# Half of the up projection by Strassen's seven block products

## Chip, cores and metric

The kernel runs on one core of a Trainium2 chip. Its time is the device time of one launch in microseconds (us), a median of several runs; lower is better.

## What is computed

One layer of a hybrid encoder on 256 tokens of width 2048: an input projection feeds chunked attention, a diagonal state-space mixer (S5) and an mLSTM; the gated branches are merged, projected and added to x; cross-attention to 256 memory tokens follows, and at the end a gated feed-forward part, which the change touches:

```python
def _swiglu(h, w_gu, w_down):
    g, u = jnp.split(h @ w_gu, 2, axis=-1)
    return (jax.nn.silu(g) * u) @ w_down
...
x = x + _swiglu(_rms(x, norm_ffn[i]), w_gu[i], w_down[i])
```

All arrays are float32; w_gu is 2048 x 11264, w_down 5632 x 2048. On the chip the 256 tokens are two token tiles of 128, and the 2048 rows of w_gu are 16 k-tiles of 128.

## The kernel before

**One product** is `gemm_i` (L120). The activations are the stationary operand, 128 k by 128 tokens; the weights move, 512 columns at a time. To keep float32 accuracy, each operand is the sum of two parts in the type float32r: a high part, the rounded value, and a low part, the rest. A product takes three matmuls: high by high (L146), high by low (L147), low by high (L148), added up in PSUM. For 512 columns and 16 k-tiles that is 16 x 2 token tiles x 3 = 96 matmuls of 512 columns.

**The weights** come from HBM in blocks of four k-tiles, 1 MB, by `load_w` (the DMA is at L101, on the queue of SP) into `raw`, which has two buffers. `split_w` (L110) makes the two parts of each half of a block, called a piece here: two k-tiles, 1024 columns wide in SBUF. ScalarE writes the high part `whi` (the cast, L116), and VectorE the low part `wlo`, raw minus high (the difference, L117):

```python
hi = wp.tile([P, 1024], F32R, tag="whi", name=nm("whi"), bufs=4)
lo = wp.tile([P, 1024], F32R, tag="wlo", name=nm("wlo"), bufs=4)
with tc.high_priority(offset=WPRI):
    S.copy(hi[:, :n], raw[:, c0:c1])
    V.tensor_tensor(lo[:, :n], raw[:, c0:c1], hi[:, :n].bitcast(F32), ALU.subtract)
```

Each has four buffers, so a piece can be made while three earlier ones wait or are read; its cast waits until TensorE has read the piece four before it.

**The feed-forward part** (from L993) has eleven chunks of 512 hidden columns. For each: `gemm_i` for the gate, its result through silu on ScalarE (L1006) into `gt`; `gemm_i` for the up projection, whose result VectorE multiplies into `gt` (L1010); then `to_operand` (L804) transposes `gt` on TensorE (L812) and splits it (L206, L207) into `hT`, the operand of the down projection with 44 k-tiles. After all eleven, four products of w_down follow, and VectorE adds x1 to each result (L1022) and stores it. A gate product and the up product of the same chunk are called a pair here. The operand of gate and up, `x2T`, is made by `to_operand` while the output projection of the cross-attention (w_xo) runs, just ahead of the feed-forward part; there VectorE adds x to its result (L844).

**The order** on each engine is set when the program is built: a scheduler takes the instructions by priority (loads, casts and differences of weights first, then what empties PSUM), and at run time every engine goes through its own list in sequence, each instruction waiting for its semaphores.

Of the kernel before, what the change touches and what calls it, by code (L numbers as in the profile page):

```python
# [9 lines left out]
F32 = mybir.dt.float32  # L10
F32R = mybir.dt.float32r
I32 = mybir.dt.int32
BF16 = mybir.dt.bfloat16
AF = mybir.ActivationFunctionType
# [4 lines left out]
P = 128  # L19
T = 256  # L20
# [11 lines left out]
KF = FF // P  # L32
# [6 lines left out]
# columns of the array of per-partition parameters  # L39
# [8 lines left out]
# columns of the array of constants: identity, ones, mask of the mLSTM  # L48
# [4 lines left out]
def tile_block(ctx: ExitStack, tc: tile.TileContext, a: dict, out: bass.AP):  # L53
# [52 lines left out]
    def dma_after(dst, src):  # L106
        """a load that comes behind the weights asked for so far"""
        with tc.issue_after(last_w[0]):
            nc.sync.dma_start(dst, src)

# [9 lines left out]
    def gemm_i(xh, xl, nk, src, off, n, evac, first=None):  # L120
        """acc[tok, n] = x @ w; w comes from the flat array src at off, in blocks [P, 4, n]."""
# [73 lines left out]
    def rstd_of(dst, ss, n, r=None):  # L195
        """dst = (ss / n + eps) ^ -0.5 (* r, one factor per partition)"""
# [6 lines left out]
    def split_act(hi, lo, src, g=None):  # L203
        """hi + lo = src * g, exactly up to float32."""
# [7 lines left out]
    def transposes(dst, srcs):  # L212
        """dst [P, len * 128] in PSUM: each src [rows, 128] transposed."""
# [10 lines left out]
    # the tensor engine's clock rises while it waits for the first loads  # L224
# [12 lines left out]
    def load_x(k, n=0):  # L237
        """what is wanted of x before the weights of k-tiles k .. k+n-1 of the first product"""
# [20 lines left out]
    def vexp(dst, src, n):  # L259
# [12 lines left out]
        # 2^k in two factors  # L272
# [12 lines left out]
    # =====================  S5  =====================  # L285
# [25 lines left out]
    def s5_params():  # L311
# [5 lines left out]
        # reduce the angle to [-pi, pi]  # L317
# [10 lines left out]
        # (a - 1) / lambda  # L328
# [50 lines left out]
    def powers(tb, c1, s1):  # L379
        """tb[:, :, j, t] = (cos, sin) of t * angle, t < 16; returns nothing."""  # L380
# [4 lines left out]
        for n, m in ((2, 1), (3, 2), (5, 4), (9, 7)):  # L385
            # entries n .. n+m-1 are those 1 .. m turned by entry n-1
# [13 lines left out]
    def s5_gen():  # L400
        """the scan, pair of groups by pair of groups; yields after each step of work"""
# [69 lines left out]
    # =====================  mLSTM  =====================  # L471
# [23 lines left out]
    def mqk(h):  # L495
        """q^T and k^T of head h, [e, tok]"""
# [26 lines left out]
    def m_gates():  # L523
        """decays of the mLSTM: a (tok-major), -c (rows), exp(-m) (tok-major)"""
# [98 lines left out]
    # =====================  chunked attention  =====================  # L623
# [60 lines left out]
    # =====================  gates and branches  =====================  # L684
# [3 lines left out]
    def gate(b, n, dst):  # L688
        """sigmoid of the gate's pre-activation, branch b, columns of chunk n, into dst(t)"""
# [37 lines left out]
    # us  # L727
# [9 lines left out]
    # xm  # L737
# [10 lines left out]
    # vm, with the input and forget gates beside head 0  # L748
# [7 lines left out]
    # attention and om  # L756
# [18 lines left out]
    # gates and branches m and a  # L775
# [30 lines left out]
    def to_operand(srcs, dh, dl, k0, gname=None):  # L806
        """srcs: two tiles [128 tok, 512]; their transpose goes to k-tiles k0 .. k0+3"""
# [328 lines left out]
```

## Time and profile before

| what | value |
|---|---|
| time, median of 3 runs | 2051.26 us (2050.34 to 2051.73) |
| profiled execution, first to last instruction (span) | 2048.7 us |
| busy: TensorE (PE) | 2039.7 us, 100% |
| busy: weight loads of TensorE (PEld) | 1670.9 us, 82% |
| busy: VectorE (DVE) | 1251.7 us, 61% |
| busy: ScalarE (ACT) | 966.0 us, 47% |
| gate and up, all eleven pairs | 1294.1 to 1797.0 us of the span |

The profile is of one execution; its own time is given by the span alone, which leaves out what lies before the first instruction and after the last. The median of the runs is 2.6 us above it. Matmuls overlap in the pipeline and their ends are modelled, so a rate is read from the distance between their starts, not from their durations.

### The profile page before, as it was taken

The page shows a single profiled execution, that of the slowest core. Times are in us where ns is not written, and L with a number is a line of the kernel's source. Part 1 is how long each engine was busy: PE and PEld are TensorE (multiplying, and loading weights), DVE is VectorE, ACT ScalarE, POOL GpSimd, SP SyncE. Part 2 cuts the span into 40 slices and gives each one's busy share as a digit, 9 for nine tenths or more (in the row PEclk, how much of TensorE's full clock was granted, in tenths as well). Part 3 has the DMA queues.
Part 4 walks back from the last instruction along what each step waited for, and adds up shares of the span by engine and source line. Part 5 has one row for each costly group of instructions (what it writes and reads, how often), then busy time and mean ns, then how long its engine had stood idle before and what let it go on. Part 6 is the DMA issues. An engine that isn't in the chain of part 4 may idle for free.

```text
span 2048.7 us, 25114 instructions
## 1 busy us (share of the span) xinstructions
PE 2039.7 (100%) x9880; PEld 1670.9 (82%) x9880; DVE 1251.7 (61%) x1804; ACT 966.0 (47%) x1308; POOL 73.7 (4%) x142
## 2 busy tenths in 40 slices
PE   9999999999999999999999999999999999999999
PEld 7998888777777788888888888888888888888887
DVE  7967885769887857645544655445444444444443
ACT  8555556544344445554544545444444444433332
POOL 1001202000000000011000100000000000000000
PEclk9999999999999999999999999999999999999999
DMA  8555455445555555765555444555555555555553
GB/s 309 186 174 165 152 179 186 155 172 174 180 183 188 192 171 195 271 218 175 175 185 185 144 145 164 185 185 185 185 185 185 185 185 185 185 185 195 195 197 132
DMA packets 60406, 377.78 MB, mean 184 GB/s; under 512 B 6912, under 2 KB 8064, under 8 KB 18816
## 3 DMA queue, kind: packets, MB, share of 16 engines
q1 hardware_dynamic: 56880, 367.42, 51.4%
q0 software_dynamic: 2112, 6.82, 1.2%
q10 hardware_dynamic: 1296, 1.95, 0.3%
q8 instruction: 77, 1.26, 0.2%
q14 instruction: 41, 0.34, 0.1%
HBM read 374.06 MB, written 2.10 MB: 184 GB/s over the span
## 4 chain that ended last, share of the span: by engine, by line
PE 99%; DVE 0%; DMA 0%; issue 0%; SPq 0%; ACT 0%; DVEq 0%; ACTq 0%
PE acc L146 29%; PE acc L148 29%; PE acc L147 28%; PE acc L169 2%; PE acc L170 2%; PE acc L171 2%; PE sm L422 1%; PE sm L812 1%; PE sm L952 1%; PE sm L978 1%; PE sm L449 1%; PE sm L215 0%; PE sm L896 0%; DMA raw<-in_w_in_dram 0%; DVE xT_l L210 0%
## 5 line engine op out<-in xcount | busy, mean ns | idle before, releaser
L117 DVE TENSOR_TENSOR wlo<-raw,whi 128x1024 fp32r<-128x1024 f32 (+2 forms) x700 | 834.7, 1194 | 697.7 <-ACT whi L116 694.3
L116 ACT CAST whi<-raw 128x1024 fp32r<-128x1024 f32 (+2 forms) x700 | 715.9, 1025 | 941.3 <-PE acc L148 816.9
L146 PE MATMUL acc<-whi,x2T_h 128*128 128x512 f32 x704 | 281.2, 399 | 0.0
L148 PE MATMUL acc<-whi,x2T_l 128*128 128x512 f32 x704 | 277.9, 395 | 0.0
L147 PE MATMUL acc<-wlo,x2T_h 128*128 128x512 f32 x704 | 277.2, 394 | 0.0
L147 PE MATMUL acc<-wlo,xT_h 128*128 128x512 f32 (+2 forms) x704 | 264.6, 377 | 1.8 <-DVE wlo L117 1.6
L148 PE MATMUL acc<-whi,xT_l 128*128 128x512 f32 (+2 forms) x704 | 265.3, 378 | 0.0
L146 PE MATMUL acc<-whi,xT_h 128*128 128x512 f32 (+2 forms) x704 | 262.4, 377 | 0.2
L148 PEld LDWEIGHTS acc<-whi,x2T_l 128*128 128x128 f32 x704 | 132.2, 188 | 33.4
L147 PEld LDWEIGHTS acc<-wlo,x2T_h 128*128 128x128 f32 x704 | 132.2, 188 | 31.4
L146 PEld LDWEIGHTS acc<-whi,x2T_h 128*128 128x128 f32 x704 | 132.2, 188 | 30.1
L147 PEld LDWEIGHTS acc<-wlo,xT_h 128*128 128x128 f32 x704 | 132.0, 188 | 29.8 <-DVE wlo L117 3.3
L146 PEld LDWEIGHTS acc<-whi,xT_h 128*128 128x128 f32 x704 | 131.5, 188 | 29.6 <-issue 3.2
L148 PEld LDWEIGHTS acc<-whi,xT_l 128*128 128x128 f32 x704 | 132.1, 188 | 27.8 <-issue 1.9
L146 PE MATMUL acc<-whi,hT_h 128*128 128x512 f32 x352 | 139.1, 395 | 0.0
L147 PE MATMUL acc<-wlo,hT_h 128*128 128x512 f32 x352 | 139.1, 395 | 0.0
L148 PE MATMUL acc<-whi,hT_l 128*128 128x512 f32 x352 | 139.0, 395 | 0.0
L148 PE MATMUL acc<-whi,eT_l 128*128 128x512 f32 x256 | 101.6, 397 | 0.0
L147 PE MATMUL acc<-wlo,eT_h 128*128 128x512 f32 x256 | 101.4, 396 | 0.0
L146 PE MATMUL acc<-whi,eT_h 128*128 128x512 f32 x256 | 101.2, 395 | 0.0
L169 PE MATMUL acc<-xT_h,whi 128*128 128x256 f32 x352 | 99.9, 284 | 0.0
L170 PE MATMUL acc<-xT_l,whi 128*128 128x256 f32 x352 | 99.5, 283 | 0.0
(375 smaller groups left out, 2837.0 us busy)
## 6 DMA issues: line engine op xcount, KB each, us to landing
raw<-in_w_gu_dram SPq DMA_DIRECT2D x88, 1024.0 KB, 4.8
raw<-in_w_in_dram SPq DMA_DIRECT2D x68, 1024.0 KB, 4.8
raw<-in_w_down_dram SPq DMA_DIRECT2D x44, 1024.0 KB, 4.7
raw<-in_w_xkv_dram SPq DMA_DIRECT2D x32, 1024.0 KB, 4.7
raw<-in_w_ii_dram SPq DMA_DIRECT2D x22, 1024.0 KB, 5.0
raw<-in_w_out_dram SPq DMA_DIRECT2D x16, 1024.0 KB, 5.0
raw<-in_w_xq_dram SPq DMA_DIRECT2D x16, 1024.0 KB, 4.8
raw<-in_w_xo_dram SPq DMA_DIRECT2D x16, 1024.0 KB, 4.8
```

The source lines that it names most:

```text
L116: S.copy(hi[:, :n], raw[:, c0:c1])
L117: V.tensor_tensor(lo[:, :n], raw[:, c0:c1], hi[:, :n].bitcast(F32), ALU.subtract)
L146: PE.matmul(o, sh, h, start=(kt == 0), stop=False)
L147: PE.matmul(o, sh, lw, start=False, stop=False)
L148: PE.matmul(o, xl[:, kt, t * P:(t + 1) * P], h, start=False, stop=(kt == nk - 1))
L169: PE.matmul(po, h, xh[:, kt, :], start=(kt == 0), stop=False)
L170: PE.matmul(po, h, xl[:, kt, :], start=False, stop=False)
L171: PE.matmul(po, lo[:, j * P:(j + 1) * P], xh[:, kt, :], start=False, stop=(kt == nk - 1))
L422: PE.matmul(pb[:, i * T:(i + 1) * T], bT[q:q + 32, i, c, :], u[q:q + 32, c, :], start=True, stop=True, tile_position=(q, 0))
L449: PE.matmul(py[q:q + 32, :], cT[:, i, 4 * c + j, :], xs[j][:, i * T:(i + 1) * T], start=(i == 0), stop=(i == 1), tile_position=(0, q))
L812: PE.transpose(px[:, j * T + t * P:j * T + (t + 1) * P], srcs[t][:, (kp + j) * P:(kp + j + 1) * P], ident)
L952: PE.matmul(pS[:, t * T:(t + 1) * T], qx[:, qi, d, t * P:(t + 1) * P], kx[:, ki, d], start=(d + i == 0), stop=(d == 3 and i == 2))
```

## The change

Of the 16 k-tiles of gate and up, the first eight, four pieces (called ordinary below), are computed as before. The last eight form four pairs of k-tiles, and for each pair the two token tiles and two k-tiles make a 2 x 2 block matrix A (A11 and A12 are the first token tile, A21 and A22 the second), the two k-tiles and two halves of 512 columns a 2 x 2 block matrix B (b11, b12, b21, b22, 128 x 256 each). A block of the four pairs is again a piece of 1024 columns.

- **Up** is computed by seven block products in place of eight (Winograd's form of Strassen's method), summed over the four pairs. It needs sums of blocks: those of A (S1 to S4) are made once, those of B by VectorE for every chunk, in place (`wsum`, L115, four of them). Two products are kept (`kept`, L217, a copy by ScalarE), and VectorE adds and subtracts them to the results in PSUM (`v`, L238). Each product of one block is 4 pairs x 3 = 12 matmuls of 256 columns.
- **Gate** is computed by the usual eight block products (`seven=False`), as the operand now lies in blocks.
- The 2 MB of the last eight k-tiles go into a buffer of their own, `sraw`, one for gate and up together; the parts of a block are made at L202 and L203.
- The operand of the blocks and of S1 to S4 is made by `pairs_operand`; `x2S` is its second half.
- **Two parts**: six chunks, their down projection (24 k-tiles), added into x1; then five chunks and theirs (20 k-tiles), added to x1 and stored. `hT` holds at most 24 k-tiles.

```diff
-KF = FF // P
+FF_PARTS = ((0, 6), (6, 11))
...
+    def wsum(dst, src):
+        with tc.high_priority(offset=WPRI):
+            V.tensor_tensor(dst, dst, src, ALU.add)
...
+    def gemm_s(xh, xl, sop, nk, src, off, evac, seven=True):
...
+        raw = spool[0].tile([P, NS * n], F32, tag="sraw", name=nm("sraw"))
+        for i in range(2):
+            load_w(src[off:off + P * 4 * n].rearrange("(p f) -> p f", p=P), 4 * n,
+                   raw[:, i * 4 * n:(i + 1) * 4 * n])
+            off += P * 4 * n
+        rv = raw.rearrange("p (i q h c) -> p q h i c", q=2, h=2, c=256)
+        b11, b12, b21, b22 = (rv[:, q, h] for q in range(2) for h in range(2))
+
+        def parts(b):
+
+            hi = wp.tile([P, 1024], F32R, tag="whi", name=nm("whi"), bufs=4)
+            lo = wp.tile([P, 1024], F32R, tag="wlo", name=nm("wlo"), bufs=4)
+            hi, lo = (x.rearrange("p (i c) -> p i c", c=256) for x in (hi, lo))
+            with tc.high_priority(offset=WPRI):
+                S.copy(hi, b)
+                V.tensor_tensor(lo, b, hi.bitcast(F32), ALU.subtract)
+            return hi, lo
+
+        def product(o, i, b, start, stop):
+            hi, lo = b
+            for p in range(4):
+                sh, sl = sop(0, p, i), sop(1, p, i)
+                PE.matmul(o, sh, hi[:, p], start=start and p == 0, stop=False)
+                PE.matmul(o, sh, lo[:, p], start=False, stop=False)
+                PE.matmul(o, sl, hi[:, p], start=False, stop=stop and p == 3)
...
+        w21, w22, w11 = parts(b21), parts(b22), None
+        if not seven:
+            w11, w12 = parts(b11), parts(b12)
+            for t in range(2):
+                for h, q, w in ((0, 0, w11), (1, 0, w12), (0, 1, w21), (1, 1, w22)):
+                    product(c(t, h), 2 * t + q, w, False, q == 1 and h == 1)
...
+        product(c(0, 0), A12, w21, False, False)
+        product(c(0, 1), S4, w22, False, True)
+        u1 = kept(side(A11, parts(b11)))
+        v(c(0, 0), c(0, 0), u1, ALU.add)
+        wsum(b11, b12)
+        wsum(b12, b22)
+        wsum(b22, b11)
+        u5 = kept(side(S1, parts(b11)))
+        p6 = side(S2, parts(b22))
+        wsum(b21, b22)
+        v(u1, p6, u1, ALU.add)
+        v(c(0, 1), c(0, 1), u5, ALU.add)
+        v(c(0, 1), c(0, 1), u1, ALU.subtract)
+        evac(0, pp[0])
+        product(c(1, 0), A22, parts(b21), False, True)
+        p7 = side(S3, parts(b12))
+        v(c(1, 1), c(1, 1), u5, ALU.add)
+        v(u1, p7, u1, ALU.add)
+        v(c(1, 0), c(1, 0), u1, ALU.add)
+        v(c(1, 1), c(1, 1), u1, ALU.subtract)
+        evac(1, pp[1])
...
+    def pairs_operand(srcs, n, gname):
...
+            b = pS.tile([P, 8, P], F32, tag="sb", name=nm("sb"), bufs=1)
+            for q in range(2):
+                S.activation(b[:, 0:4].rearrange("p (t q) c -> p q t c", q=2)[:, q],
...
+            V.tensor_tensor(b[:, S1], b[:, A21], b[:, A22], ALU.subtract)
+            V.tensor_tensor(b[:, S3], b[:, A11], b[:, A21], ALU.subtract)
+            V.tensor_tensor(b[:, S2], b[:, S1], b[:, A11], ALU.subtract)
+            V.tensor_tensor(b[:, S4], b[:, S2], b[:, A12], ALU.add)
+            f = b.rearrange("p i c -> p (i c)")
+            split_act(sop(0, pair, 0, 8), sop(1, pair, 0, 8), f)
...
-        off = gemm_i(gTh, gTl, KD, a["w_gu"], off, 512, evg)
-        off = gemm_i(gTh, gTl, KD, a["w_gu"], off, 512, evu)
-        to_operand(sg, hTh, hTl, 4 * n)
...
+    for c0, c1 in FF_PARTS:
+        nk = 4 * (c1 - c0)
...
+            gu_off = gemm_s(gT[0], gT[1], sop, KD, a["w_gu"], gu_off, evg, seven=False)
+            gu_off = gemm_s(gT[0], gT[1], sop, KD, a["w_gu"], gu_off, evu)
+            to_operand(sg, hTh, hTl, 4 * (n - c0))
+        for n in range(4):
+            def ev(t, po, n=n, last=(c1 == FF // 512)):
+                with tc.high_priority(offset=EPRI):
+                    if not last:
+                        d = x1[:, t, n * 512:(n + 1) * 512]
+                        V.tensor_tensor(d, po, d, ALU.add)
+                        return
...
+            gemm_i(hTh, hTl, nk, a["w_down"], (n * FF + c0 * 512) * 512, 512, ev)
```

How the order changes, first on VectorE, in the up product of the second chunk. Before, differences of ordinary pieces follow each other (L117), with the two multiplications of the gate by up (L1010) among them:

```order
L117 TENSOR_TENSOR wlo_11771<-raw_11752,whi_11770 128x1024
L117 TENSOR_TENSOR wlo_11789<-raw_11786,whi_11788 128x1024
L117 TENSOR_TENSOR wlo_11805<-raw_11786,whi_11804 128x1024
L117 TENSOR_TENSOR wlo_11843<-raw_11840,whi_11842 128x1024
L117 TENSOR_TENSOR wlo_11859<-raw_11840,whi_11858 128x1024
L117 TENSOR_TENSOR wlo_11877<-raw_11874,whi_11876 128x1024
L1010 SCALAR_TENSOR_TENSOR gt_11540<-acc_11682,rst,gt_11540 128x512
L1010 SCALAR_TENSOR_TENSOR gt_11541<-acc_11683,rst,gt_11541 128x512
```
Now, line numbers being those of the changed kernel, in the same place, for the blocks of up (L203: difference of a block, L115: sum of blocks, L238: addition of a kept product `u`). `wlo_11974` is of b11, `wlo_11997` of its sum, `wlo_12016` belongs to the fifth product, `wlo_12038` and `wlo_12054` to the sixth and seventh:

```order
L203 TENSOR_TENSOR wlo_11942<-sraw_11938,whi_11941 128x1024
L203 TENSOR_TENSOR wlo_11946<-sraw_11938,whi_11945 128x1024
L203 TENSOR_TENSOR wlo_11974<-sraw_11938,whi_11973 128x1024
L115 TENSOR_TENSOR sraw_11938<-sraw_11938 128x4x256 x2
L203 TENSOR_TENSOR wlo_11997<-sraw_11938,whi_11996 128x1024
L115 TENSOR_TENSOR sraw_11938<-sraw_11938 128x4x256
L238 TENSOR_TENSOR acc_11868<-acc_11868,u_11990 128x256
L115 TENSOR_TENSOR sraw_11938<-sraw_11938 128x4x256
L203 TENSOR_TENSOR wlo_12016<-sraw_11938,whi_12015 128x1024
L238 TENSOR_TENSOR acc_11868<-acc_11868,u_12013 128x256
L203 TENSOR_TENSOR wlo_12038<-sraw_11938,whi_12037 128x1024
L203 TENSOR_TENSOR wlo_12054<-sraw_11938,whi_12053 128x1024
```
The sums and additions stand between the differences, and the addition at L238 of the kept third product is ahead of the fourth sum.

On ScalarE, from gate to up of the same chunk. Before, casts of ordinary pieces (L116) with the silu (L1006) between:

```order
L116 CAST whi_11736<-raw_11718 128x1024
L1006 ACTIVATE gt_11541<-acc_11543,rst 128x512
L116 CAST whi_11754<-raw_11752 128x1024
L116 CAST whi_11770<-raw_11752 128x1024
L116 CAST whi_11788<-raw_11786 128x1024
L116 CAST whi_11804<-raw_11786 128x1024
```
Now, from the third block of the gate's last eight k-tiles (`whi_11762`) over the split of the last chunk's `hT` and the fourth block (`whi_11766`) to the first ordinary piece of up (`whi_11872`):

```order
L202 CAST whi_11762<-sraw_11751 128x1024
L311 CAST hT_h_11267<-sm_11665 128x512
L311 CAST hT_h_11267<-sm_11672 128x512
L202 CAST whi_11766<-sraw_11751 128x1024
L122 CAST whi_11872<-raw_11870 128x1024
```
The first piece of up is the fifth buffer use after the gate's first block, so its cast comes behind the four casts of the gate's blocks.

On TensorE, at the end of the fourth product of up (`whi_11996`), the fifth (`sm_12019`) and the sixth (first into `acc_11869` with `whi_12037`). There was no such place before: `gemm_i` goes piece by piece.

```order
L212 MATMUL sm_12000<-whi_11996,x2S_l 128x256
L210 MATMUL sm_12019<-whi_12015,x2T_h 128x256
L210 MATMUL acc_11869<-whi_12037,x2T_h 128x256
L211 MATMUL sm_12019<-wlo_12016,x2T_h 128x256
L212 MATMUL sm_12019<-whi_12015,x2T_l 128x256
```
And at the end of the fifth, where the seventh (`sm_12057`) begins with one matmul, ahead of the rest of the sixth:

```order
L212 MATMUL sm_12019<-whi_12015,x2S_l 128x256
L210 MATMUL sm_12057<-whi_12053,x2T_h 128x256
L211 MATMUL acc_11869<-wlo_12038,x2T_h 128x256
L212 MATMUL acc_11869<-whi_12037,x2T_l 128x256
```
Of each later product one matmul by the high part is drawn forward; the next needs the low part of the product before it.

## Rows read from the trace of the kernel before

**Rows 1.** The page: busy time by engine, and TensorE's granted clock in forty slices.
```profile
PE 2039.7 (100%) x9880; PEld 1670.9 (82%) x9880; DVE 1251.7 (61%) x1804; ACT 966.0 (47%) x1308; POOL 73.7 (4%) x142
PEclk9999999999999999999999999999999999999999
```
**Rows 2.** The page: the chain that ended last, by engine and by line.
```profile
PE 99%; DVE 0%; DMA 0%; issue 0%; SPq 0%; ACT 0%; DVEq 0%; ACTq 0%
PE acc L146 29%; PE acc L148 29%; PE acc L147 28%; PE acc L169 2%; PE acc L170 2%; PE acc L171 2%; PE sm L422 1%; PE sm L812 1%; PE sm L952 1%; PE sm L978 1%; PE sm L449 1%; PE sm L215 0%; PE sm L896 0%; DMA raw<-in_w_in_dram 0%; DVE xT_l L210 0%
```
**Rows 3.** Busy time by stretch: PE, PEld, DVE, ACT, POOL, granted clock, DMA share, GB/s.
```profile
0.00:3.00 3.00, 1.52 (x4) 1.25 (x5) 0.71 (x6) 0.00 (x0) 0.19 (x4) 1.00 0.38 96
1294.10:1797.00 502.90, 502.90 (x2203) 405.55 (x2203) 245.00 (x225) 212.34 (x227) 1.47 (x4) 1.00 0.52 184
```
**Rows 4.** Timeline at the gate and up projections: start, duration in us, instruction.
```profile
1499.71 0.40 PE L146 MATMUL acc<-whi,x2T_h 128*128 128x512 f32 x1
...
1500.18 0.39 PE L148 MATMUL acc<-whi,x2T_l 128*128 128x512 f32 x1
...
1500.61 1.05 ACT L116 CAST whi<-raw 128x1024 fp32r<-128x1024 f32 x1 [0.71 <-PE acc L148]
...
1501.69 1.22 DVE L117 TENSOR_TENSOR wlo<-raw,whi 128x1024 fp32r<-128x1024 f32 x1 [1.58 <-ACT whi L116]
...
1507.88 0.39 PE L148 MATMUL acc<-whi,x2T_l 128*128 128x512 f32 x1
```
**Rows 5.** Instructions by line and shape, whole span: busy us, mean ns of one.
```profile
L117 DVE TENSOR_TENSOR wlo<-raw,whi 128x1024 fp32r<-128x1024 f32 x658 | 804.2, 1224 | 675.5 <-ACT whi L116 672.3
L308 DVE TENSOR_TENSOR u<-acc,rb 128x256 f32<-128x256 f32 x6 | 2.5, 425 | 1.2 <-PE acc L171 1.0
L844 DVE TENSOR_TENSOR x<-acc,x 128x512 f32<-128x512 f32 x8 | 5.1, 683 | 0.0
L362 DVE TENSOR_TENSOR s2k<-braw,s5p 128x128 f32<-128x128 f32 x6 | 1.7, 284 | 0.0
L116 ACT CAST whi<-raw 128x1024 fp32r<-128x1024 f32 x658 | 688.9, 1049 | 910.6 <-PE acc L148 809.0 <-PE acc L170 27.4 <-DMA raw<-in_w_out_dram 14.5
```
**Rows 6.** Timeline of matmuls of 256 columns and of their weight loads.
```profile
149.90 0.28 PE L146 MATMUL acc<-whi,xT_h 128*128 128x256 f32 x1
...
153.43 0.28 PE L146 MATMUL acc<-whi,xT_h 128*128 128x256 f32 x1
...
150.13 0.19 PEld L146 LDWEIGHTS acc<-whi,xT_h 128*128 128x128 f32 x1
150.25 0.19 PEld L147 LDWEIGHTS acc<-wlo,xT_h 128*128 128x128 f32 x1
```
**Rows 7.** Timeline of single short steps, at three other places.
```profile
6.18 0.69 DVE L117 TENSOR_TENSOR wlo<-raw,whi 128x512 fp32r<-128x512 f32 x1
...
6.92 0.50 PE L147 MATMUL acc<-wlo,xT_h 128*128 128x512 f32 x1 [0.35 <-DVE wlo L117]
7.26 0.39 PE L148 MATMUL acc<-whi,xT_l 128*128 128x512 f32 x1
...
60.90 0.37 ACT L369 COPY s5mats<-sm 128x256 f32<-128x256 f32 x1
...
204.35 0.42 DVE L442 TENSOR_TENSOR xx<-xx,s2k 128x256 f32<-128x256 f32 x1
204.69 0.42 DVE L443 TENSOR_TENSOR xx<-xx,s2k 128x256 f32<-128x256 f32 x1
```
**Rows 8.** DMA: rate in forty slices of the first 40 us; then the page.
```profile
GB/s 0 31 256 276 317 329 302 229 238 301 406 428 397 401 402 410 410 320 299 373 422 434 401 238 385 401 410 426 382 420 449 379 66 123 303 426 397 430 426 418
...
HBM read 374.06 MB, written 2.10 MB: 184 GB/s over the span
...
raw<-in_w_gu_dram SPq DMA_DIRECT2D x88, 1024.0 KB, 4.8
```

More of the change, by code (lines that the diff above doesn't have):

```diff
@@ L109, in dma_after @@
             nc.sync.dma_start(dst, src)
+    spool = [None]
+    def wsum(dst, src):
+        with tc.high_priority(offset=WPRI):
+            V.tensor_tensor(dst, dst, src, ALU.add)
     def split_w(raw, c0, c1):
@@ L989, in tile_block @@
                      resid_evac(n, 2, lambda t: x1[:, t, n * 512:(n + 1) * 512]))
-        to_operand([x1[:, t, n * 512:(n + 1) * 512] for t in range(2)], gTh, gTl, 4 * n,
-                   "norm_ffn")
+        srcs = [x1[:, t, n * 512:(n + 1) * 512] for t in range(2)]
+        if n < 2:
+            to_operand(srcs, gT[0], gT[1], 4 * n, "norm_ffn")
+        else:
+            pairs_operand(srcs, n - 2, "norm_ffn")
     finish_rstd(2, 6)
-    p2.release()
     poolA.release()
     p3 = tc.alloc_tile_pool(name="p3", bufs=1)
-    hTh = p3.tile([P, KF, T], F32R, name="hT_h")
@@ L999, in tile_block @@
-    hTl = p3.tile([P, KF, T], F32R, name="hT_l")
-    off = 0
-    for n in range(FF // 512):
-        sg = [t2k("gt", 2), t2k("gt", 2)]
-        def evg(t, po, sg=sg):
-            with tc.high_priority(offset=EPRI):
-                S.activation(sg[t], po, AF.Silu, scale=rst[:, 6 + t:7 + t])
-        def evu(t, po, sg=sg):
-            with tc.high_priority(offset=EPRI):
-                V.scalar_tensor_tensor(sg[t], po, rst[:, 6 + t:7 + t], sg[t], ALU.mult, ALU.mult)
-        off = gemm_i(gTh, gTl, KD, a["w_gu"], off, 512, evg)
-        off = gemm_i(gTh, gTl, KD, a["w_gu"], off, 512, evu)
-        to_operand(sg, hTh, hTl, 4 * n)
@@ L1014, in tile_block @@
-    off = 0
-    for n in range(4):
-        def ev(t, po, n=n):
-            o = t2k()
-            with tc.high_priority(offset=EPRI):
-                for c in range(0, 512, 256 if n == 3 else 512):
-                    d = slice(c, c + (256 if n == 3 else 512))
-                    g = slice(n * 512 + d.start, n * 512 + d.stop)
-                    V.tensor_tensor(o[:, d], po[:, d], x1[:, t, g], ALU.add)
-                    (nc.sync if c else nc.scalar).dma_start(out[t * P:(t + 1) * P, g], o[:, d])
-        off = gemm_i(hTh, hTl, KF, a["w_down"], off, 512, ev)
+    spool[0] = p3
@@ new lines, in tile_block, with evg, evu @@
+    gu_off = 0
+    for c0, c1 in FF_PARTS:
+        nk = 4 * (c1 - c0)
+        hTh = p3.tile([P, nk, T], F32R, tag="hh", name=nm("hT_h"))
+        hTl = p3.tile([P, nk, T], F32R, tag="hl", name=nm("hT_l"))
+        for n in range(c0, c1):
+            sg = [t2k("gt", 2), t2k("gt", 2)]
+            def evg(t, po, sg=sg):
+                with tc.high_priority(offset=EPRI):
+                    S.activation(sg[t], po, AF.Silu, scale=rst[:, 6 + t:7 + t])
+            def evu(t, po, sg=sg):
+                with tc.high_priority(offset=EPRI):
+                    V.scalar_tensor_tensor(sg[t], po, rst[:, 6 + t:7 + t], sg[t], ALU.mult,
+                                           ALU.mult)
+            gu_off = gemm_s(gT[0], gT[1], sop, KD, a["w_gu"], gu_off, evg, seven=False)
[3 more added lines that the diff above has]
+            def ev(t, po, n=n, last=(c1 == FF // 512)):
+                with tc.high_priority(offset=EPRI):
+                    if not last:
+                        d = x1[:, t, n * 512:(n + 1) * 512]
+                        V.tensor_tensor(d, po, d, ALU.add)
+                        return
+                    o = t2k()
+                    for c in range(0, 512, 256 if n == 3 else 512):
+                        d = slice(c, c + (256 if n == 3 else 512))
+                        g = slice(n * 512 + d.start, n * 512 + d.stop)
+                        V.tensor_tensor(o[:, d], po[:, d], x1[:, t, g], ALU.add)
+                        (nc.sync if c else nc.scalar).dma_start(out[t * P:(t + 1) * P, g],
+                                                                o[:, d])
+            gemm_i(hTh, hTl, nk, a["w_down"], (n * FF + c0 * 512) * 512, 512, ev)
@@ L1025, in tile_block @@
     p3.release()
+    pS.release()
     px1.release()
```

55 lines of the change are left out of this document (53 added, 2 removed).

## Prediction

> **What bounds the kernel now.** I read the page first: busy time by engine, then the chain that ended last, then the stretch of the gate and up projections, then single instructions there. [rows 1, 2] TensorE is busy for 2039.7 of 2048.7 us and is 99% of the chain: nothing else ends late anywhere, so a microsecond of TensorE work saved is a microsecond of time, and a wait put before it is one lost. In the stretch of the 11 gate/up pairs (502.9 us, 45.7 a pair) TensorE is busy throughout, VectorE for 245.0 and ScalarE for 212.3 us [rows 3]. So both have half their time free, but that is an average; what counts is whether a weight piece is ready when TensorE comes to it. [rows 4] show the present beat: 36 matmuls of 512 columns start from 1499.71 to 1507.88, 0.2334 us apart, so a piece of two k-tiles (12 matmuls) takes 2.80 us. The last matmul that reads a piece starts at 1500.18; the cast into its buffer starts at 1500.61, 0.20 after TensorE's next start; the difference follows 0.03 after the cast. Cast and difference take 1.05 and 1.22 us per 1024 columns [rows 5], 2.3 of 2.8 us, with four buffers each: the pieces run three ahead and TensorE never sees them.
>
> **The work on TensorE.** A matmul of 256 columns starts every 0.1177 us (31 from 149.90 to 153.43, each with its own weight load) [rows 6]: half of 512 within 1%, so halving the width costs almost nothing. Gate: 48 matmuls of 512 become 96 of 256: 11.30 for 11.20 us, +0.10. Up: 48 become 84 of 256 (seven products of 12, in place of eight): 9.89 for 11.20, -1.31. The order shows that these counts are really there. Without new waits a pair gains 1.21 us, 13.3 us over eleven.
>
> **The waits, up.** Call 0 the start of the first of the seven products; they take 1.41 us each. The third block's cast reuses the buffer of the third ordinary piece, which TensorE leaves at -2.80; with the 0.20 above it runs from -2.60 to -1.55, its difference to -0.30. Only then may b11 be overwritten: two sums on VectorE. No row has such a sum (1024 columns in four strips, in place). Its bounds are one difference of 1024 columns back to back, 1.14 us (1.22 less the 0.08 by which neighbours overlap), and four adds of 256 columns at 0.42, 1.68 us [rows 5, 7]; I take 1.22, since the differences of the same blocks have the same count and type. The two end at 2.10, the difference of the new b11 at 3.30 (its cast ended at 2.05), the third sum at 4.44. VectorE's next instruction adds the kept third product: that ends on TensorE at 4.24, +0.20, +0.37 for the ScalarE copy [rows 7], so the add runs 4.83 to 5.25 (0.42 [rows 5]). The fourth sum ends at 6.39, the difference for the fifth product at 7.53. TensorE ended the fourth product at 5.65 and has two first-part matmuls (0.24) that need no difference; the rest starts at 7.58 (0.05 from difference to matmul, and about 0.1 more for the first matmul after a wait: 0.34 instead of 0.23 [rows 7]). That is an idle 1.7 + 0.1 = **1.8 us**. The other two differences end at 9.01 and 10.15, before TensorE wants them (9.09 and 10.85). The order of the three queues decides this: each is in sequence, the add stands ahead of the fourth sum, and TensorE has only one matmul each of the next products to go on with.
>
> **The waits, gate to up.** The gate holds its four blocks to the end, because both token tiles use each. The first ordinary piece of up reuses the buffer of the third block, free only after seven of eight products: 84 x 0.1177 + 0.20 = 10.09, cast to 11.14, difference to 12.39, matmul at 12.44. The gate's products ended at 11.30 and one matmul of 0.23 goes ahead: idle 0.91, with the restart **1.0 us**. At the other boundary, up to gate, the first buffers are freed by products long done; nothing is late there.
>
> **Work at nothing.** The additions of kept products after the last product, the silu and the eight extra adds of the first feed-forward part into x1 (0.68 each [rows 5]) fall under ordinary pieces, where VectorE and ScalarE have half their time; the transposes of a pair stand 5 us after its last product, and the chain before them (an add, two differences, two adds, the gating) is about as long, which leaves no more than 0.2 us. The down projection has as many matmuls as before, in 24 + 20 k-tiles. **Loads**: the block buffer of 2 MB is single, and SP issues the next two loads only when the last difference or sum has read it: 10.15 after 0. At the 400 GB/s that the queue reached in the first 40 us, 2.1 MB takes 5.2 us, and an issue-to-landing of 4.8 for 1 MB leaves some 2.2 fixed [rows 8]: landed at 17.6, third cast done at 20.8 to 21.6, while TensorE has the ordinary pieces and transposes until 23.8. Cover 2 us; if it were gone, the wait would follow microsecond for microsecond.
>
> **Once**: the first gate. Its operand for the last k-tile pair is made behind the cast of the fourth block, which waits for the last ordinary piece. From the start of the products: 0.2, cast 1.05, difference 1.22, four sums of 128 columns at 0.28, cast 1.05, difference 1.22 = 5.9 [rows 5]. TensorE has 22 matmuls (2.6 us) that need less: **3.3 us**.
>
> **Sum.** A pair: +0.10 - 1.31 + 1.8 + 1.0 = +1.6; eleven +17.5; with the 3.3, **+20.8 us**. The profiled execution's span is 2048.7, so 2069.5; the runs' median stands 2.6 above the span, so 2072. All hops shorter (sums at 1.14, no restart costs) give +14; sums at 1.68 give 1.8 us more a pair, +41.
>
> **Rivals.** (a) *The blocks are ready in time.* Then the products show their count: 11 x -1.21 + 3.3 = -10, 2041 us. For it: VectorE is idle half the time. Against: the chain above has no slack in it, since every link waits for a buffer or a sum, not for a free engine. The point where it decides: waits per pair must fall from 2.8 to under 1.2 for no loss, to 0.5 to be seen as faster. 0.08; half-way, within the measurement, 0.05. (b) *The block loads come late.* At the mean rate of 184 GB/s [rows 8] 2.1 MB takes 11.4 us, landing is at 23.8 and the third block's difference at 28.2: 4.4 us per pair, 2120. Against it, the queue holds nothing else at that time. 0.04. (c) *The clock falls in the waits.* All forty slices have the full clock, 2.4 GHz, and so has the first 3 us, where TensorE had stood idle for half [rows 1, 3]. Were the last three products of up (36 matmuls) granted 1.2 GHz, they would take 4.2 us longer, 46 in all: 2118. 0.04. (d) *Weight loads become the bound.* A pair's products have 180 loads where 96 were; at the 0.19 us shown for one, laid end to end, 34.2 us for 22.4, +130: 2181. But [rows 6] loads of 0.19 start every 0.118 us, so they overlap. 0.02. The Trainium skill, Perfetto Trace Analysis, section Identifying the Most-Contended Engine, says to judge TensorE's headroom by the busy share of the weight loads, not of the matmuls. By that rule the change spends what is scarce and (d) would come; by the row the loads have room for 256 columns, and the sum stands.
>
> **The numbers.** My forecast has 0.77, and its own range is 2065 to 2092, from the bounds of the sums and hops. Cases (b) to (d) lie above, 0.10; (a) and its half-way case below, 0.13. The range of eight in ten is 2056 to 2092. A difference under 0.2%, 4.1 us, can't be told from none: faster 0.08, same 0.05, slower 0.87.
>
> **What would show it.** Right: TensorE's idle time, nearly none today, comes to some 34 us, in twenty-two pieces, with the difference of the fifth product's block and that of up's first piece as releasers; a pair takes about 47.3 us; VectorE is busy without a gap for 10 us around the products of up; 256-column matmuls start 0.118 apart. Wrong: no such gaps (a); gaps ended by DMA (b); a clock slice under 9 (c); 256-column matmuls 0.19 apart (d). If the waits are shorter than 1.2 us a pair, the step that failed is the chain of sums.

## The result and the profile after

| | before | changed |
|---|---|---|
| median of the runs, us | 2051.49 (2050.34 to 2052.85, 4 runs) | 2067.35 (2066.55 to 2068.12, 4 runs) |
| span of the profiled execution, us | 2048.7 | 2065.9 |

The ratio is 1.0078 (95% interval 1.0064 to 1.0092): 15.9 us slower, where 20.8 were forecast. The first fence is the page of the changed kernel: busy time by engine, granted clock, the chain that ended last, the loads of the block buffer.

```profile
PE 2037.9 (99%) x10804; PEld 1711.8 (83%) x10804; DVE 1377.2 (67%) x1989; ACT 1007.0 (49%) x1367; POOL 73.9 (4%) x142
...
PEclk9999999999999999999999999999999999999999
...
PE 95%; DVE 2%; DMA 1%; ACT 1%; issue 0%; DVEq 0%; ACTq 0%; SPq 0%
...
sraw<-in_w_gu_dram SPq DMA_DIRECT2D x44, 1024.0 KB, 6.8
```

Against [rows 1, 2] TensorE's busy time hardly moved (2039.7 to 2037.9), the clock is full throughout, and the chain now has some 4% of other engines in it. So TensorE computes no more than before; it waits. The view of its waits, in the feed-forward part, says where (instruction, who ended the wait, us in total, times, longest):

```profile
PE acc L210 <- ACT whi L202: 15.3, 11, 1.4
PE acc L210 <- ACT x2S_h L311: 1.4, 1, 1.4
PE acc L211 <- DVE wlo L203: 1.0, 2, 0.8
PE acc L212 <- DVE x2S_l L312: 0.5, 1, 0.5
```

Eleven waits for the cast of a block, one a pair; of the four others three stand at the first gate and one, the shorter of its line, in the fifth pair. The timeline at the second pair's up products, TensorE first, then VectorE, then ScalarE:

```profile
1380.93 0.28 PE L210 MATMUL acc<-whi,x2T_h 128*128 128x256 f32 x1
...
1386.57 0.27 PE L212 MATMUL sm<-whi,x2S_l 128*128 128x256 f32 x1
1386.82 0.38 PE L210 MATMUL sm<-whi,x2T_h 128*128 128x256 f32 x1
1388.59 0.39 PE L210 MATMUL acc<-whi,x2T_h 128*128 128x256 f32 x1 [1.39 <-ACT whi L202]
1388.82 0.28 PE L211 MATMUL sm<-wlo,x2T_h 128*128 128x256 f32 x1
...
1380.67 2.49 DVE L115 TENSOR_TENSOR sraw<-sraw 128x1024 f32<-128x1024 f32 x2
1383.09 1.23 DVE L203 TENSOR_TENSOR wlo<-sraw,whi 128x1024 fp32r<-128x1024 f32 x1
1384.23 1.22 DVE L115 TENSOR_TENSOR sraw<-sraw 128x1024 f32<-128x1024 f32 x1
1385.85 0.43 DVE L238 TENSOR_TENSOR acc<-acc,u 128x256 f32<-128x256 f32 x1 [0.40 <-ACT u L217]
1386.19 1.22 DVE L115 TENSOR_TENSOR sraw<-sraw 128x1024 f32<-128x1024 f32 x1
1387.32 1.22 DVE L203 TENSOR_TENSOR wlo<-sraw,whi 128x1024 fp32r<-128x1024 f32 x1
...
1385.44 0.37 ACT L217 COPY u<-sm 128x256 f32<-128x256 f32 x1 [2.39 <-PE sm L212]
1385.71 1.05 ACT L202 CAST whi<-sraw 128x1024 fp32r<-128x1024 f32 x1
1386.88 0.37 ACT L217 COPY u<-sm 128x256 f32<-128x256 f32 x1
1387.49 1.99 ACT L202 CAST whi<-sraw 128x1024 fp32r<-128x1024 f32 x2 [0.24 <-DVE sraw L115]
```

VectorE works on without a break except the 0.40 us in which it stands before the add of the kept product. The fourth sum ends at 1387.41; from there both the cast of one block (start 1387.49) and the difference of another (1387.32 to 1388.54) run, both end at about 1388.54, and TensorE goes on at 1388.59. Its two starts are 1.77 apart in place of 0.12; with 0.13 lost ahead of the first and 0.11 at the restart that is 1.89 us.

The boundary from gate to up, where a second wait was forecast. The gate's products start at 1404.88:

```profile
1407.84 0.40 PE L210 MATMUL acc<-whi,x2T_h 128*128 128x256 f32 x2
...
1416.35 0.28 PE L212 MATMUL acc<-whi,x2S_l 128*128 128x256 f32 x1
1416.47 0.39 PE L185 MATMUL acc<-whi,x2T_h 128*128 128x512 f32 x1
1416.71 0.40 PE L186 MATMUL acc<-wlo,x2T_h 128*128 128x512 f32 x1
...
1408.03 1.05 ACT L122 CAST whi<-raw 128x1024 fp32r<-128x1024 f32 x1 [1.51 <-PE acc L212]
```

No gap: the first ordinary piece was cast at 1408.03, 8.4 us before TensorE wanted it. It is 0.19 after the start of 1407.84, when the gate's first 24 block matmuls were through: the order on TensorE uses one block for both token tiles first, and its buffer is free then. It is not the block that was filled first. At the first gate, where the blocks come late, the first matmul by a low part (1309.14, shown next) starts 0.05 us after the third difference of a block ends, although the first two had ended at 1306.82:

```profile
1304.46 2.36 DVE L203 TENSOR_TENSOR wlo<-sraw,whi 128x1024 fp32r<-128x1024 f32 x2 [0.84 <-ACT whi L202]
...
1307.87 1.22 DVE L203 TENSOR_TENSOR wlo<-sraw,whi 128x1024 fp32r<-128x1024 f32 x1
```

The three waits that come once are at the first gate; the rows with what preceded them:

```profile
1307.99 0.40 PE L210 MATMUL acc<-whi,x2T_h 128*128 128x256 f32 x2
1309.14 0.39 PE L211 MATMUL acc<-wlo,x2T_h 128*128 128x256 f32 x1 [0.76 <-DVE wlo L203]
...
1311.05 0.28 PE L212 MATMUL acc<-whi,x2S_l 128*128 128x256 f32 x1
1312.73 0.38 PE L210 MATMUL acc<-whi,x2S_h 128*128 128x256 f32 x1 [1.41 <-ACT x2S_h L311]
...
1313.20 0.27 PE L211 MATMUL acc<-wlo,x2S_h 128*128 128x256 f32 x1
1313.99 0.38 PE L212 MATMUL acc<-whi,x2S_l 128*128 128x256 f32 x1 [0.52 <-DVE x2S_l L312]
```

Each start less the normal spacing (two matmuls ahead of the first): 0.91, 1.56 and 0.67, 3.1 us in all. With about 0.1 us more at each of the three restarts, this gate takes 14.98 us where the next takes 11.52: 3.5 us, paid once.

**The account.** A pair takes 46.75 us (from 1341.84 to 1388.59) against 45.69 before, 1.06 more. Its gate products run from 1358.21 to the next ordinary matmul:

```profile
1358.21 0.40 PE L210 MATMUL acc<-whi,x2T_h 128*128 128x256 f32 x2
...
1369.73 0.40 PE L185 MATMUL acc<-whi,x2T_h 128*128 128x512 f32 x1
```

The parts, from starts: 96 gate matmuls in 11.52 (11.20 before), +0.32; 84 up matmuls at 0.120, 10.08, -1.12; the wait, +1.89. That is +1.09. (The gate at 1404.88 above takes 11.59 because it starts right behind a transpose: its second matmul starts 0.20 after its first. Five of the eleven gates take 11.52; the transposes cost the same elsewhere, since the pairs are equally long.) Eleven periods are 11.7; with the 3.5 of the first gate and one more wait in the fifth pair, 0.5, the sum is 15.7. The feed-forward part, from its first matmul to the last of the kernel, grew by 15.7. The runs differ by 15.9, the profiled spans by 17.2; 1.5 of the spans' difference lies ahead of the feed-forward part, which the change hardly touches: the part starts at 1295.9 here, at 1294.4 in the trace of the kernel before, and between 1294.4 and 1295.9 in the runs below.

### The profile page after: what moved, and what is told of

Read it like the earlier page. It is cut to its first block, busy times and chain, and to the rows that moved or that the text cites. A ratio compares the mean times of both kernels' runs of the same rounds, so it can differ in the third digit from the quotient of the medians.

```text
span 2065.9 us, 27248 instructions
## 1 busy us (share of the span) xinstructions
PE 2037.9 (99%) x10804; PEld 1711.8 (83%) x10804; DVE 1377.2 (67%) x1989; ACT 1007.0 (49%) x1367; POOL 73.9 (4%) x142
## 4 chain that ended last, share of the span: by engine, by line
PE 95%; DVE 2%; DMA 1%; ACT 1%; issue 0%; DVEq 0%; ACTq 0%; SPq 0%
PE acc L152 20%; PE acc L154 20%; PE acc L153 20%; PE acc L187 4%; PE acc L186 4%; PE acc L185 4%; PE acc L210 3%; PE acc L212 3%; PE acc L211 3%; PE acc L274 2%; PE acc L275 2%; PE acc L276 2%; PE sm L527 1%; PE sm L917 1%; PE sm L212 1%; PE sm L211 1%
## 5 line engine op out<-in xcount | busy, mean ns | idle before, releaser
L123 DVE TENSOR_TENSOR wlo<-raw,whi 128x1024 fp32r<-128x1024 f32 (+2 forms) x612 | 725.3, 1189 | 511.3 <-ACT whi L122 509.6
L122 ACT CAST whi<-raw 128x1024 fp32r<-128x1024 f32 (+2 forms) x612 | 622.1, 1022 | 717.4 <-PE acc L154 530.0
L203 DVE TENSOR_TENSOR wlo<-sraw,whi 128x1024 fp32r<-128x1024 f32 x121 | 146.0, 1223 | 80.2 <-ACT whi L202 80.2
L202 ACT CAST whi<-sraw 128x1024 fp32r<-128x1024 f32 x121 | 124.6, 1047 | 149.0 <-PE acc L187 76.3
L187 PE MATMUL acc<-whi,x2T_l 128*128 128x512 f32 x352 | 139.7, 397 | 0.0
L186 PE MATMUL acc<-wlo,x2T_h 128*128 128x512 f32 x352 | 139.6, 397 | 0.0
L185 PE MATMUL acc<-whi,x2T_h 128*128 128x512 f32 x352 | 132.7, 395 | 0.0
L276 PE MATMUL acc<-xT_h,wlo 128*128 128x256 f32 x352 | 99.2, 282 | 0.0
```

The source lines that it names most:

```text
L185: PE.matmul(pp[t], sh, h, start=(kt == 0), stop=False)
L186: PE.matmul(pp[t], sh, lw, start=False, stop=False)
L187: PE.matmul(pp[t], xl[:, kt, t * P:(t + 1) * P], h, start=False, stop=False)
L203: V.tensor_tensor(lo, b, hi.bitcast(F32), ALU.subtract)
L276: PE.matmul(po, lo[:, j * P:(j + 1) * P], xh[:, kt, :], start=False, stop=(kt == nk - 1))
```

## The experiments

Theory: the loss is the chain of sums on VectorE, the spacing of the gate's 256-column matmuls, and the first gate's operand. Rivals stand with each run. Base is the changed kernel unless said. Times are medians; the ratio is to the kernel before on the same chip.

**No sums.**

```diff
     def wsum(dst, src):
-        with tc.high_priority(offset=WPRI):
-            V.tensor_tensor(dst, dst, src, ALU.add)
+        return
```

> The changed kernel without the four block sums on VectorE (this leaves out part of the computation: the up projection's seven products use the unsummed weight blocks). Theory 'chain of sums': the gap of TensorE in the seven products of up, 1.65 us from start to start beyond the normal spacing and with its restarts 1.88 us a pair, comes from four sums and a copy-and-add that stand in one queue on VectorE. Without the sums it goes: 2067.4 - 11 x 1.88 = about 2047 us, and TensorE's idle time behind the block casts (15.3 us) falls to under 2 us. Rival 'buffers': the wait is set by the four part buffers and by the 1.05 us casts on ScalarE; then the sums only lie beside it and the time stays within 4 us of 2067.

2045.75 us, 0.9972 (0.9961 to 0.9984): 21.6 less than with them. The waits for block casts are gone from the view; of 15.3 us none is left. The rival falls.

**Another order of the seven products.**

```diff
-        product(c(0, 0), A12, w21, False, False)
-        product(c(0, 1), S4, w22, False, True)
         u1 = kept(side(A11, parts(b11)))
-        v(c(0, 0), c(0, 0), u1, ALU.add)
         wsum(b11, b12)
+        product(c(0, 0), A12, parts(b21), False, False)
+        product(c(0, 1), S4, parts(b22), False, True)
         wsum(b12, b22)
         wsum(b22, b11)
         u5 = kept(side(S1, parts(b11)))
-        p6 = side(S2, parts(b22))
+        p7 = side(S3, parts(b12))
         wsum(b21, b22)
+        p6 = side(S2, parts(b22))
+        v(c(0, 0), c(0, 0), u1, ALU.add)
...
         product(c(1, 0), A22, parts(b21), False, True)
-        p7 = side(S3, parts(b12))
```

> All of the computation, but the seven products of up in another order: A11 by b11 first (so that b11 and b12 are summed while the last ordinary pieces run), the product of S3 ahead of that of S2, the product that needs the fourth sum last, the first add behind the fourth sum. Theory 'chain of sums': it is the place of the sums, not their length, that costs; the sums then begin some 8 us earlier and end before TensorE wants them, the 1.88 us a pair go: 2067.4 - 20.7 = about 2047 us (2046 to 2052), no gap over 0.2 us in the products of up. Rival 'VectorE has no room': seven differences and four sums, 13 us of VectorE in 10 us of products, cannot be hidden by order; the wait moves to another product and the time stays over 2060.

2046.46 us, 0.9975 (0.9965 to 0.9985), all of the computation done: 20.9 us less than the changed kernel, 1.90 a pair, and below the kernel before. VectorE and TensorE at the second pair, whose products start at 1379.40:

```profile
1373.54 1.23 DVE L115 TENSOR_TENSOR sraw<-sraw 128x1024 f32<-128x1024 f32 x1
...
1376.23 1.22 DVE L115 TENSOR_TENSOR sraw<-sraw 128x1024 f32<-128x1024 f32 x1
...
1379.14 1.23 DVE L115 TENSOR_TENSOR sraw<-sraw 128x1024 f32<-128x1024 f32 x1
...
1381.87 1.22 DVE L115 TENSOR_TENSOR sraw<-sraw 128x1024 f32<-128x1024 f32 x1
...
1379.40 0.28 PE L210 MATMUL sm<-whi,x2T_h 128*128 128x256 f32 x1
...
1388.16 0.63 PE L185 MATMUL acc<-whi,x2T_h 128*128 128x512 f32 x2
```

The same four sums; three of them now start ahead of the products, the first 5.9 us ahead. The 73 block matmuls before the next ordinary one take 8.76 us; in the changed kernel as many took 10.64 (1380.93 to 1391.57). The difference is the wait. A pair now takes 44.86 us, 1.89 less than in the changed kernel. So it was not the amount of VectorE's work but its place.

**Without the first add.** One line is left out: `v(c(0, 0), c(0, 0), u1, ALU.add)`.

> The changed kernel without the one VectorE instruction that adds the kept third product to the result (this leaves out part of the computation: that product is missing in the first quarter of up). In the changed kernel this add stands ahead of the fourth block sum and the queue stands still 0.40 us for it and works 0.43 us on it. Theory 'chain of sums': the wait of TensorE shrinks by these 0.83 us a pair: 2067.4 - 11 x 0.83 = about 2058 us, a gap of about 0.8 us left in every pair. Rival 'buffers': an add of 256 columns matters only for its own place; the gap stays 1.65 us and the time within 2 us of 2067.

2063.24 us, 1.0058 (1.0043 to 1.0073): 4.1 less, neither the 9 expected nor nothing. The fourth sum was done 0.70 us earlier beside TensorE's clock, as meant, but the timeline of ScalarE shows the next limit:

```profile
1385.35 1.05 ACT L202 CAST whi<-sraw 128x1024 fp32r<-128x1024 f32 x1
1386.52 0.37 ACT L217 COPY u<-sm 128x256 f32<-128x256 f32 x1
1386.79 2.00 ACT L202 CAST whi<-sraw 128x1024 fp32r<-128x1024 f32 x2
```

The copy of the fourth product stands ahead of the cast that TensorE waits for, and it must itself wait for TensorE. Two runs followed to see whether this queue is the second limit.

**Without copies and additions.** `kept` and `v` do nothing.

> The changed kernel without the copies of the kept products and without the additions of products to the results (this leaves out part of the computation: three of the seven products of up are computed and not used). It follows on the run without the first add, which gave 4.1 us and not the 9 expected. Theory 'two queues': there the sums were done 0.7 us earlier, but the cast that TensorE waits for stood behind the copy of the fourth product on ScalarE (ended 1386.89, the cast follows without idle time). Without the copies that cast can start at the end of the fourth sum, 0.39 us earlier: 2063.2 - 11 x 0.39 = about 2059 us, and what is left of the wait, some 1.1 us a pair, is that of the sums alone. Rival 'sums only': the copies do not matter, the time stays at 2063.

2066.64 us, 1.0077 (1.0060 to 1.0094): no help, and the run does not answer its question. With the additions gone, up's gating has nothing to wait for but the first products, and it took the place of the add in VectorE's queue, between the third sum and the fourth (at the next pair):

```profile
1429.21 1.22 DVE L115 TENSOR_TENSOR sraw<-sraw 128x1024 f32<-128x1024 f32 x1
1430.35 0.74 DVE L1148 SCALAR_TENSOR_TENSOR gt<-acc,rst,gt 128x512 f32<-128x512 f32 x1
1431.01 1.22 DVE L115 TENSOR_TENSOR sraw<-sraw 128x1024 f32<-128x1024 f32 x1
```

From the start of the third sum to that of the fourth it is 1.80 us here, 1.96 in the changed kernel, and 1.26 without the first add, where nothing stands between: the gating costs 0.54 us, not much less than the 0.70 of the add and its wait. TensorE's waits for casts are 15.4 us again. What the copies cost is not shown by this run.

**Without the first add and the fourth copy.** As the run without the first add, and:

```diff
-        u5 = kept(side(S1, parts(b11)))
+        side(S1, parts(b11))
...
-        v(c(0, 1), c(0, 1), u5, ALU.add)
...
-        v(c(1, 1), c(1, 1), u5, ALU.add)
```

> The run without the first add, and besides without the copy of the kept fourth product and its two additions (this leaves out part of the computation: two of up's seven products are missing in some quarters); the gating of up stays behind the products. In the run without the first add the cast that TensorE waited for started at 1386.79, right at the end of that copy, 0.39 us after the cast ahead of it (ended 1386.40) and 0.44 after the fourth sum (1386.35). Theory 'two queues' (ScalarE is the second limit, 0.4 us behind VectorE): the cast starts 0.39 us earlier, 2063.2 - 11 x 0.39 = about 2059 us, a gap of some 1.1 us left. Rival 'sums only': the copy does not matter, 2063 us.

2059.71 us, 1.0041 (1.0027 to 1.0055): 3.5 less than without the first add alone, 4.3 expected. The copy was the second limit, 0.3 to 0.4 us behind the first. The wait had two nearly equal ends, and taking 0.8 us from one gave 0.4.

**Gate by 512 columns.**

```diff
-            w11, w12 = parts(b11), parts(b12)
-            for t in range(2):
-                for h, q, w in ((0, 0, w11), (1, 0, w12), (0, 1, w21), (1, 1, w22)):
-                    product(c(t, h), 2 * t + q, w, False, q == 1 and h == 1)
+            for i in range(4):
+                hi, lo = split_w(raw, 2 * i * n, 2 * (i + 1) * n)
+                for t in range(2):
+                    for q in range(2):
...
+                        PE.matmul(pp[t], sh, h, start=False, stop=False)
...
```

> All of the computation, but the gate's last eight k-tiles by 512-column matmuls, one pair of k-tiles after the other, in place of eight products of 256-column blocks. Theory 'spacing': 256-column matmuls of the products start 0.1207 us apart and 512-column ones 0.2334, so a gate gets 11.59 - 11.20 = 0.39 us back, 4.3 over eleven; and the first gate needs the operand of the last pair only after three quarters of its matmuls, so the once paid 3.2 us go: 2067.4 - 7.5 = about 2060 us. Rival 'halving is free': the spacing of 0.1177 seen before holds and the rest of a pair's loss lies in other places: only the 3.2 us go, and 1 us for the count: 2063 us or more.

2059.47 us, 1.0038 (1.0023 to 1.0053): 7.9 less, 7.5 expected. The three waits at the first gate are gone from the view of waits. The 0.1207 in the expectation holds for a gate behind a transpose; from the traces the gain is 0.32 x 11 = 3.5, the first gate's 3.5 and the fifth pair's 0.5, which is 7.5 as well.

**Eight products for up too.** The up call gets `seven=False`.

> The changed kernel with the usual eight products for up as for gate: the blocks, their operand and the 256-column matmuls are there, the sums and the saving are not. Theory 'spacing': 2 x 96 matmuls of 256 columns take 2 x 11.59 us a pair against 2 x 11.20, so 0.78 x 11 = 8.6, and the first gate's 3.2 us: 2051.4 + 11.8 = about 2063 us, no gap at the boundaries. Rival 'halving is free': 2 x 0.10 x 11 + 3.2 = 2057 us.

2062.35 us, 1.0052 (1.0037 to 1.0067): 10.9 over the kernel before, 11.8 expected, 5.4 by the rival, which falls. The sum of the theory is close, its parts are not. A pair takes 46.32 us, 0.63 more than before and not 0.78: twice the 0.32 of a gate. The rest lies at the first gate, which takes 16.47 us, 1.5 more than in the changed kernel with the same three waits. Behind them TensorE's granted clock was 0.50, the level of 1.2 GHz, for 3.4 us, and matmuls started 0.213 us apart. Busy time (PE, PEld, DVE, ACT, POOL), granted clock, DMA share and GB/s there:

```profile
1314.00:1317.30 3.30, 3.30 (x18) 3.30 (x17) 0.00 (x0) 0.00 (x0) 0.00 (x0) 0.50 0.72 300
```

Narrow matmuls without Strassen's saving cost what their spacing says, 7.0 us over eleven pairs.

**Feed-forward in two parts alone**, in the kernel before.

> The kernel before with one part of the change alone: the feed-forward in two parts, six chunks and five, each with its down projection. Theory: it costs nothing, the eight additions into x1 lie beside TensorE's work: 2051.4 us, within 2. Rival 'the second start': a transposed operand that must be ready before the first down projection, twice in place of once, costs some us: 2054 or more.

2050.88 us, 0.9998 (0.9989 to 1.0008): nothing.

**Blocks held to the end.** The gate's 96 matmuls with the pairs of k-tiles outermost:

```diff
-            for t in range(2):
-                for h, q, w in ((0, 0, w11), (1, 0, w12), (0, 1, w21), (1, 1, w22)):
-                    product(c(t, h), 2 * t + q, w, False, q == 1 and h == 1)
+            blocks = ((0, 0, w11), (1, 0, w12), (0, 1, w21), (1, 1, w22))
+            for p in range(4):
+                for t in range(2):
+                    for h, q, (hi, lo) in blocks:
...
```

> All of the computation, but the gate's 96 block matmuls go through the four pairs of k-tiles outermost, so that every block is read until the last 12 matmuls of 96 and the first buffer comes free after 87. Theory 'order of release': the wait between gate and up that was forecast at 1.0 us a pair did not come because the order of the products lets go of one block after 24 matmuls, and the next cast takes that buffer. Held to the end, the cast starts at 87 x 0.1207 + 0.2 = 10.7, the difference ends at 13.0, where TensorE wants it at 12.06 (96 products and two matmuls that need no difference): about 1.0 us with the restart, 11 a launch. The last pair's operand is needed later, so the 3.2 us paid once go: 2067.4 + 11 - 3 = about 2076 us. Rival 'the buffers do not matter there' (the casts run ahead anyway): no gap at that place, only the 3.2 us go: 2064 us.

2095.63 us, 1.0214 (1.0197 to 1.0231): 28 more where 9 were expected. TensorE at the second gate's start and at the boundary to up:

```profile
1409.89 0.27 PE L232 MATMUL acc<-whi,x2T_l 128*128 128x256 f32 x1
1410.59 0.50 PE L230 MATMUL acc<-whi,x2T_h 128*128 128x256 f32 x2 [0.42 <-ACT whi L202]
1411.85 0.39 PE L231 MATMUL acc<-wlo,x2T_h 128*128 128x256 f32 x1 [0.76 <-DVE wlo L203]
...
1422.39 0.28 PE L232 MATMUL acc<-whi,x2S_l 128*128 128x256 f32 x1
1422.94 0.73 PE L185 MATMUL acc<-whi,x2T_h 128*128 128x512 f32 x2 [0.27 <-ACT whi L122]
1424.20 0.50 PE L186 MATMUL acc<-wlo,x2T_h 128*128 128x512 f32 x1 [0.53 <-DVE wlo L123]
```

At the boundary the forecast wait is there: starts 0.55 and 1.26 apart where 0.12 and two of 0.23 are normal, and 0.34 for 0.23 at the restart, 1.3 us against some 1.0. The rest was not foreseen: this order wants all four blocks within the first twelve matmuls, so the last one's cast and difference are late at the gate's start (0.70 and 1.26 for 0.12 and 0.24), 1.6 us more. This pair is 3.0 us longer than in the changed kernel. Where transposes stand ahead of the gate only one of the two waits at its start is left, and a pair is 2.4 longer. The first pair is 2.3 longer: the operand's waits are gone there, but these are in their place. Together 29 us, as measured in the feed-forward part.

**Both cures.** The new order and the gate by 512 columns.

> Both cures: up's products in the order that begins with A11 by b11, and the gate by 512-column matmuls. If the two are separate costs they add: 2046.5 - 7.9 = about 2038.5 us, below the kernel before by 13 us, which is 11 times the saving of 84 matmuls of 256 columns at 0.1204 us against 11.20 us (1.09 a pair, 12.0). Rival 'the time saved brings the next wait' (loads of the block buffer, 2 us of cover; casts): over 2042 us.

2038.59 us, 0.9936 (0.9921 to 0.9951): 12.8 below the kernel before, as expected; no wait of TensorE is left in the whole feed-forward part.

**Gate by seven products too**, with the new order.

> All of the computation; the gate too by the seven products, in the order that begins with A11 by b11. TensorE's work falls by 1.48 us a pair against the run with the new order alone (84 x 0.1204 in place of 96 x 0.1207): if VectorE and the loads keep up, 2046.5 - 16.3 = about 2030 us. Against it: VectorE then has 8 sums, 14 block differences, 8 ordinary differences and 12 additions a pair and two products with their sums 23 us apart; some 37 us of 43. Rival 'VectorE becomes the bound': waits of TensorE behind sums or differences come back in both products, 2046 or more.

2054.85 us, 1.0018 (1.0009 to 1.0028): the rival. Busy time by engine in 100 us of it (PE, PEld, DVE, ACT):

```profile
1330.00:1430.00 100.00, 98.51 (x610) 87.67 (x609) 94.20 (x109) 58.39 (x68) 0.00 (x0) 1.00 0.47 188
```

VectorE is busy for 94 of 100 us and can no longer be ahead; TensorE waits 24 times for casts after the first pair, 15.4 us, and 5.2 us in the first. Around these the granted clock was 0.50 for 6.8 us.

## Why the prediction was right, and where not

Sign and size were right: 2067.35 in a range of 2056 to 2092, 5 us under the forecast. That the sum came so close is partly luck: one of its two waits was not there, and two smaller errors made up for half of it. Of the 34 us of waits that were to be seen in twenty-two pieces, 24 came, in eleven pieces of 1.89 and at the first gate. By its steps:

- **The chain of sums: right.** Forecast 1.8 us a pair, measured 1.89. The runs without the sums and with the new order show that it is the sums, by their place. With the products' start as 0 the first two sums were to end at 2.10, the third at 4.44, the fourth at 6.39, the difference behind it at 7.53; by the fences above they end at 2.23, 4.52, 6.48 and 7.61. The sum, a kind of instruction that no row before had shown, took 1221 ns, as the difference of the same size did in [rows 5]; the strips cost nothing. (The Trainium skill, Vector Engine (DVE) Microarchitecture Reference, section 5.2 Measured stream behaviour on trn2, gives 1.04 ns a column and about 75 ns an instruction for operations of one or two sources, an estimate of 1.14 us here; the fourth sum and its follower start 1.13 apart.) One detail was off. The forecast lets two first-part matmuls go ahead; only one could, since the second is the sixth product's and needs the cast of the block that the fourth sum makes. This cast on ScalarE ends the wait, and the forecast comes out because it ends within 0.05 us of the difference that was reckoned with.
- **The gate to up wait: wrong.** The step that failed is "The first ordinary piece of up reuses the buffer of the third block, free only after seven of eight products". It took the buffers in the order in which they were filled, and every block as held to the end; the cast got the one that the gate let go first, that of the block filled third, after 24 of 96 matmuls. 11 us of the forecast fell away. The run with the blocks held shows that the wait itself was priced fairly (1.3 against 1.0) and was there to be had.
- **The spacing of 256 columns: right in kind, too small.** Forecast 0.1177 from [rows 6], measured 0.120 in gate and up. A gate loses 0.32, not 0.10; up gains 1.12, not 1.31. Together 0.41 a pair, 4.5 us. One stretch of 31 matmuls was little to go by: in the kernel before, other even stretches of 256 columns ran at 0.1167 (108 matmuls from 759.12) to 0.1187, and none was as slow as the blocks.
- **The first gate: right**, 3.5 for 3.3.
- **Work at nothing: right.** The two parts cost nothing by themselves, and no wait of TensorE in the feed-forward part is ended by a load.
- **The rivals.** (a) did not come, but the new order shows that it could: the forecast's "no slack in it, since every link waits for a buffer or a sum" holds for this order alone. (b) is excluded by the waits. (c) did not come in the changed kernel, whose granted clock was 1.00 in all eleven pairs; but the sign named for it, a clock slice under 9, could not have shown a short fall. A slice is 52 us, and the 3.4 us at 0.50 in the run with eight products left every slice at 9. (d): during the gate's products the busy time of the weight loads fills the whole window, and still matmuls start 0.12 apart and not 0.19. The rule cited there (the Trainium skill, Perfetto Trace Analysis, section Identifying the Most-Contended Engine), as far as it goes by the weight loads' busy share, would see no headroom in this row; the measured spacing decides against it:

```profile
1404.88:1416.47 11.59, 11.59 (x99) 11.59 (x98) 5.03 (x6) 5.49 (x7) 0.00 (x0) 1.00 0.48 181
```

So 11 us too much at the boundary stand against 4.5 too little in the spacing and 1 in the chain of sums.

## What to carry to other kernels

A saving on the bounding engine is real only if the helper work that it needs can start before the engine arrives: lay the helper's queue out in time, instruction by instruction, and put products that feed a chain first and those that use its end last. When a wait is shortened, replay the other queues too, since the next limit may be 0.4 us behind. Before pricing a buffer wait, look up in the order of the readers which buffer is let go first, not which was filled first.

## What the hardware showed that was not expected

- Matmuls of 256 columns in the block products start 0.120 us apart; in the kernel before even stretches of the same width ran at 0.1167 to 0.1187, and half of 512 columns is 0.1167. Loads, clock and shapes are the same in the rows. Neither the sums nor the waits are the cause: without sums, and with eight products for up, it is 0.120 too. The cause stays open. The 512-column gate shows only that the cost goes with the width.
- A TensorE that starts again after a wait shows 0.38 to 0.39 us for its first 256-column matmul where 0.28 is normal, and the next one starts 0.23 us after it in place of 0.12: 0.11 us more for each wait.
- The clock can fall around waits of a microsecond or two. In five of the profiled executions (no sums, the new order, eight products, blocks held, seven for the gate too) the granted clock was 0.50, the level of 1.2 GHz, for one stretch of 3.4 us in the first pair, 6.8 in the last of them. In the run with eight products TensorE's starts had been 1.05, 1.68 and 0.80 us apart in the six microseconds before, and the fall cost 1.5 us. In the changed kernel they were 1.04, 1.68 and 0.80 apart at the same place, and the clock stayed at 1.00. What decides it stays open.
